# Attention scores of two transformer blocks: mask and biases added on VectorE instead of TensorE, 64-row key products padded to 128 rows

## The chip, the cores and the metric

The program runs on one core of a Trainium2 chip. The metric is device time in microseconds (us); runs of this kernel lie within about 0.1% of each other. The engines are TensorE (PE, with its weight loads PEld), VectorE (DVE), ScalarE (ACT), GpSimd (POOL) and SyncE (SP), each with its own instruction queue; they meet through semaphores.

## What is computed

Two transformer blocks on 256 tokens of width 2048, in fp32. Cut to the attention, which is what the change touches:

```python
# first block: 16 MLA heads (128 plain + 64 rotated dimensions) and 16 FoX heads (128 dimensions)
s = q @ k.T * Dk ** -0.5                    # Dk = 192 (MLA) or 128 (FoX)
s = s + F[t] - F[s']                        # FoX only: cumulative log of the forget gates
s = where(key <= query, s, -inf)
y = softmax(s) @ v
# first block goes on: gates, output projection, 16384 experts (PEER)

# second block, two layers: 4 differential heads, 8 dilated heads, a convolution
s_c = q_c @ k_c.T * 64 ** -0.5 + bias[dist] # c = 0, 1: two score maps of 64 dimensions per head
a = softmax(s_0) - lam * softmax(s_1);  y = rms_norm(a @ v)
s = q @ k.T * 128 ** -0.5 + bias[dist] + log(count of patterns)   # dilated heads, 128 dimensions
y = softmax(s) @ v
```

## The kernel before

Almost all of the program is a list of jobs. A job takes a weight block of 512 by 512 numbers from DRAM (1 MB) and cuts it into four pieces of 128 by 512. ACT rounds a piece to a high part `hi` (L204), DVE subtracts to get the low part `lo` (L205), and PE multiplies: for each of two token blocks the three products hi*h, lo*h, hi*l (L256, L257, L259), so six matmuls of 512 columns per piece. Pieces are converted up to `PIECES` = 7 ahead of the matmuls. SP loads the next blocks.

Everything else (norms, heads, rotations, the convolution) is a generator in a task list. After each piece the planner (`Tasks.step`) lets one task per lane take one step if it is due; what the step issues is then queued on the engines behind what is there. A step that yields a number waits for so many pieces; a bare `yield` waits four. PE's queue is thus a stream of main matmuls with short runs of other matmuls, called sites here, between two pieces.

An attention head is three sites. The first makes the score tile `sc` in PSUM with `qk` (first block, L561 to L569) or `qk_plain` (second block, L1092 to L1094): queries 0 to 127 against keys 0 to 127, and queries 128 to 255 against keys 0 to 255, 384 columns in all. An fp32 matmul stands in the trace as two records. In the first block `qk` adds the forget sums with a 48-row matmul (`extra`, L593: three copies of 16 rows, picked by `sel`) and the causal mask with a bf16 matmul of the identity and the mask (L569). An MLA head has a second product for its 64 rotated dimensions; two heads share one transposed tile of 128 rows, so the head takes rows 0 to 63 or 64 to 127 of it (`rows`, in `mla_group`). The differential heads take their two maps in the same way from a tile of 128 rows (`rows`, in `diff_post`).

Behind the site, `softmax_block` takes the maxima on DVE (L521, L522), negates them (L523), and ACT makes the exponentials and their sums (L524, L525). In the second block `biased` first adds the position bias on DVE from PSUM into SBUF (L1088, L1089), so that the maxima and exponentials read SBUF there and PSUM in the first block. The second site (four or more pieces later) transposes the weights, the third multiplies by the values.

POOL's queue carries the small loads of the first block: the forget bias, a triangle of ones, and the gate biases (L712). A task `forget_work` makes the forget sums `F` once.

## Time and profile before

| | |
|---|---|
| median of 3 runs | 3363.84 us (3362.52 to 3364.47) |
| profiled execution | 3362.86 us, of which the span of the trace is 3361.1 us |
| PE busy | 99% of the span |
| PEld, DVE, ACT, POOL busy | 81%, 70%, 53%, 17% |
| chain that ended last | PE 95%, DVE 3%, ACT 1%, DMA 1%, issue 1% |
| mean granted TensorE clock | 0.997 of full speed |

The page shows busy shares and the chain of work that ended last. A busy PE is not PE at its peak, since matmuls overlap in its pipeline: a record of a main matmul lasts about 0.39 us, but the next one starts 0.23 us after it. What a matmul costs the stream is therefore read from the distance of the starts in the timeline, not from the length of a record.

### The profile page before, as it was taken

The page shows a single profiled execution, that of the slowest core. Times are in us where ns is not written, and L with a number is a line of the kernel's source. Part 1 is how long each engine was busy: PE and PEld are TensorE (multiplying, and loading weights), DVE is VectorE, ACT ScalarE, POOL GpSimd, SP SyncE. Part 2 cuts the span into 40 slices and gives each one's busy share as a digit, 9 for nine tenths or more (in the row PEclk, how much of TensorE's full clock was granted, in tenths as well). Part 3 has the DMA queues.
Part 4 walks back from the last instruction along what each step waited for, and adds up shares of the span by engine and source line. Part 5 has one row for each costly group of instructions (what it writes and reads, how often), then busy time and mean ns, then how long its engine had stood idle before and what let it go on. Part 6 is the DMA issues. An engine that isn't in the chain of part 4 may idle for free.

```text
span 3361.1 us, 43418 instructions
## 1 busy us (share of the span) xinstructions
PE 3327.9 (99%) x15371; PEld 2737.1 (81%) x15372; DVE 2338.2 (70%) x4597; ACT 1772.8 (53%) x3117; POOL 558.1 (17%) x489
## 2 busy tenths in 40 slices
PE   9999999999999999999999999999999999999997
PEld 7877888888888888888888888888887888788886
DVE  6676676666778877444567677767668777778877
ACT  6655554554555555555554444444555454455453
POOL 0000000000007777877021111110000000000001
PEclk9999999999999999999999999999999999999999
DMA  6434444578547777777676666665564445444454
GB/s 241 163 138 155 174 163 164 192 236 286 197 176 213 210 198 213 213 207 213 235 276 240 247 237 237 237 240 214 198 220 163 163 170 199 173 162 161 176 188 138
DMA packets 157754, 674.46 MB, mean 201 GB/s; under 512 B 50384, under 2 KB 67152, under 8 KB 85984
## 3 DMA queue, kind: packets, MB, share of 16 engines
q1 hardware_dynamic: 102416, 613.06, 51.9%
q0 software_dynamic: 54688, 58.33, 7.3%
q8 instruction: 120, 1.97, 0.2%
q14 instruction: 98, 0.80, 0.1%
q10 hardware_dynamic: 432, 0.29, 0.0%
HBM read 633.48 MB, written 38.14 MB: 200 GB/s over the span
## 4 chain that ended last, share of the span: by engine, by line
PE 95%; DVE 3%; ACT 1%; DMA 1%; issue 1%; SPq 0%; DVEq 0%; ACTq 0%
PE acc L256 29%; PE acc L259 29%; PE acc L257 29%; PE side L226 2%; PE side L566 1%; DVE lo L205 1%; PE side L1094 1%; DMA raw<-in_win_dram 1%; PE side L531 0%; PE side L540 0%; PE side L541 0%; PE side L542 0%; PE side L569 0%; PE side L593 0%; PE side L832 0%
## 5 line engine op out<-in xcount | busy, mean ns | idle before, releaser
L205 DVE TENSOR_TENSOR lo<-raw,hi 128x512 fp32r<-128x512 f32 x2244 | 1505.4, 688 | 787.9 <-ACT hi L204 779.5
L204 ACT CAST hi<-raw 128x512 fp32r<-128x512 f32 x2244 | 1371.4, 622 | 1140.9 <-DVE lo L205 621.5
L256 PE MATMUL acc<-hi,xh 128*128 128x512 f32 x2816 | 1120.7, 398 | 2.0 <-ACT xh L1350 0.9
L259 PE MATMUL acc<-hi,xl 128*128 128x512 f32 x2816 | 1099.4, 391 | 3.0 <-DVE xl L205 2.8
L257 PE MATMUL acc<-lo,xh 128*128 128x512 f32 x2816 | 1098.7, 390 | 3.5 <-DVE lo L205 3.5
L256 PE MATMUL acc<-hi,s 128*128 128x512 f32 x1664 | 653.2, 393 | 0.6 <-ACT hi L204 0.6
L257 PE MATMUL acc<-lo,s 128*128 128x512 f32 x1664 | 647.8, 389 | 0.6 <-DVE lo L205 0.6
L259 PE MATMUL acc<-hi,s 128*128 128x512 f32 x1664 | 646.3, 390 | 0.0
L259 PEld LDWEIGHTS acc<-hi,xl 128*128 128x128 f32 x2816 | 529.3, 188 | 116.7 <-DVE xl L205 4.1
L256 PEld LDWEIGHTS acc<-hi,xh 128*128 128x128 f32 x2816 | 529.9, 188 | 112.6 <-issue 5.7
L257 PEld LDWEIGHTS acc<-lo,xh 128*128 128x128 f32 x2816 | 530.3, 188 | 109.2 <-DVE lo L205 5.5
L907 POOL DMA_INDIRECT gd<-pick x256 | 427.4, 1669 | 93.0 <-issue 74.5
L259 PEld LDWEIGHTS acc<-hi,s 128*128 128x128 f32 x1664 | 312.3, 188 | 65.4
L257 PEld LDWEIGHTS acc<-lo,s 128*128 128x128 f32 x1664 | 312.6, 188 | 64.3 <-DVE lo L205 1.3
L256 PEld LDWEIGHTS acc<-hi,s 128*128 128x128 f32 x1664 | 312.6, 188 | 64.2 <-ACT hi L204 1.5
L1327 POOL TENSOR_TENSOR X<-X,s 128x512 f32<-128x512 f32 x6 | 9.0, 1528 | 888.7 <-ACT X L1326 888.7
L1215 DVE SCALAR_TENSOR_TENSOR s<-s,vec,s 128x256 f32<-128x256 f32 x240 | 115.4, 481 | 4.6
L712 POOL DMA_DIRECT2D s<-in_bgate_dram x8 | 4.3, 538 | 676.4 <-ACT hi L204 421.4
L945 POOL DMA_DIRECT2D s<-ad x32 | 17.1, 534 | 482.6 <-PE acc L259 482.6
L937 POOL DMA_DIRECT2D ad<-s x32 | 27.4, 857 | 403.4 <-ACT s L935 403.4
L226 PE MATMUL side<-cst,s 128*128 128x128 f32 x720 | 92.6, 272 | 0.0
L226 PEld LDWEIGHTS side<-cst,s 128*128 128x128 f32 x720 | 83.6, 140 | 10.7
(269 smaller groups left out, 1807.0 us busy)
## 6 DMA issues: line engine op xcount, KB each, us to landing
raw<-in_ut_dram SPq DMA_DIRECT2D x128, 1024.0 KB, 4.9
raw<-in_pv_dram SPq DMA_DIRECT2D x128, 1024.0 KB, 4.8
raw<-in_w_dram SPq DMA_DIRECT2D x120, 1024.0 KB, 4.8
raw<-in_win_dram SPq DMA_DIRECT2D x87, 1024.0 KB, 5.0
raw<-in_wout_dram SPq DMA_DIRECT2D x32, 1024.0 KB, 5.0
raw<-in_wo_dram SPq DMA_DIRECT2D x32, 1024.0 KB, 4.8
gd<-s SPq DMA_DIRECT2D x16, 1024.0 KB, 8.7
raw<-in_wpq_dram SPq DMA_DIRECT2D x16, 1024.0 KB, 4.8
```

The lines of the kernel that those rows point to most:

```text
L204: A.copy(out=hi, in_=src)
L205: V.tensor_tensor(out=lo, in0=src, in1=hi.bitcast(F32), op=OP.subtract)
L226: PE.transpose(pv[:, i, tb * P:(tb + 1) * P], src_of(c + i, tb), ident)
L256: PE.matmul(ps[tb], lhsT=lh[:, kc, t], rhs=wh, start=start, stop=False)
L257: PE.matmul(ps[tb], lhsT=lh[:, kc, t], rhs=wl, start=False, stop=False)
L259: PE.matmul(ps[tb], lhsT=ll[:, kc, t], rhs=wh, start=False, stop=stop)
L566: PE.matmul(o, lhsT=q[:, q0:q0 + P], rhs=k[:, 0:k1], start=i == 0, stop=False)
L907: G.indirect_dma_start(out=gd.rearrange("p (n o) -> (p n) o", o=1), out_offset=bass.IndirectOffsetOnAxis(ap=pick[:, 1, h, k:k + 1].bitcast ...
L937: G.dma_start(out=S["ad", g], in_=aT.rearrange("p j t -> p (j t)"))
L945: G.dma_start(out=aT.rearrange("p j t -> p (j t)"), in_=S["ad", g])
L1094: PE.matmul(sc[:, o0:o0 + k1], lhsT=q[:, q0:q0 + P], rhs=k[:, 0:k1], start=True, stop=True)
L1215: V.scalar_tensor_tensor(out=cv[:, c], in0=pad[:, k:k + T], scalar=tapw(k), in1=cv[:, c], op0=OP.mult, op1=OP.add)
```

## The change

The forget sums are written to DRAM once (`fd`), and for each group of four FoX heads a new task, `forget_bias`, loads them back spread over all 128 partitions and adds the mask. The MLA heads get a fixed mask tile `causal`. Every score tile is then read by one DVE instruction per part that adds mask or bias, writes the sum to SBUF and keeps its maximum; ACT's exponentials read SBUF everywhere. The 48-row and the identity matmuls go. For the 64-row products the key side is stored twice, multiplied by a column `halves` that is 1 on one half of the rows and 0 on the other, and the product runs over all 128 rows.

```diff
-    identb = kept([128], BF16, "identb")
-    maskb = kept([128], BF16, "maskb")
-    V.tensor_copy(out=identb, in_=ident)
-    V.tensor_copy(out=maskb, in_=maskf)
+    causal = kept([384], name="causal")
+    V.memset(causal[:, 128:256], 0.0)
+    for c0 in (0, 256):
+        V.tensor_copy(out=causal[:, c0:c0 + 128], in_=maskf)
+    halves = kept([2], name="halves")
+    V.tensor_reduce(out=halves, in_=ident.rearrange("p (a b) -> p a b", a=2), axis=AX.X, op=OP.add)
...
-        F = kept([T], F32R, "F", 48)
-        A.activation(out=F, in_=pf, func=AF.Copy, scale=-1.0)
-        V.scalar_tensor_tensor(out=F[32:48], in0=pf[32:48], scalar=-1.0, in1=F[32:48].bitcast(F32), op0=OP.mult,
-                               op1=OP.subtract)
-        S["F"] = F
+            PE.matmul(pf, lhsT=lf[:, tb], rhs=tri[:, tb, :], start=tb == 0, stop=tb == TB - 1)
+        F = s2([T])
+        A.activation(out=F[0:16], in_=pf, func=AF.Copy, scale=-1.0)
+        G.dma_start(out=S["fd"], in_=F[0:16])
+        yield END
+
+    def forget_bias(g):
+
+        f, f0 = s4([4, T]), s2([4, P])
+        G.dma_start(out=f.rearrange("p h t -> p (h t)"), in_=row_bcast(S["fd"], 4 * g * T, 4 * T))
+        yield 8
+        mask = maskf[:, None, :].to_broadcast([P, 4, P])
+        V.tensor_tensor(out=f0, in0=f[:, :, 0:P], in1=mask, op=OP.add)
+        V.tensor_tensor(out=f[:, :, P:T], in0=f[:, :, P:T], in1=mask, op=OP.add)
+        S["fbias", g] = (f0, f)
         yield END
...
-    def softmax_block(src, sums, nmax, fresh=False):
-
-        pr = s2([384]) if fresh else src
-        mx = small(2)
-        V.tensor_reduce(out=mx[:, 0:1], in_=src[:, 0:128], axis=AX.X, op=OP.max)
-        V.tensor_reduce(out=mx[:, 1:2], in_=src[:, 128:384], axis=AX.X, op=OP.max)
+    def softmax_block(sc, b0, b1, sums):
+
+        pr = s2([384])
+        mx, nmax = small(2), small(2)
+        parts = ((slice(0, 128), b0), (slice(128, 384), b1))
+        for i, (c, bias) in enumerate(parts):
+            V.tensor_tensor_reduce(out=pr[:, c], in0=sc[:, c], in1=bias, scale=1.0, scalar=-3.0e38, op0=OP.add,
+                                   op1=OP.max, accum_out=mx[:, i:i + 1])
...
-    def qk(sc, parts, extra=None):
+    def qk(sc, parts):
 
         for q0, k1, o0 in ((0, P, 0), (P, T, P)):
-            o = sc[:, o0:o0 + k1]
             for i, (q, k) in enumerate(parts):
-                PE.matmul(o, lhsT=q[:, q0:q0 + P], rhs=k[:, 0:k1], start=i == 0, stop=False)
-            if extra:
-                extra(o, k1)
-            PE.matmul(o[:, k1 - P:k1], lhsT=identb, rhs=maskb, start=False, stop=True)
+                PE.matmul(sc[:, o0:o0 + k1], lhsT=q[:, q0:q0 + P], rhs=k[:, 0:k1], start=i == 0,
+                          stop=i == len(parts) - 1)
...
+            keys["f"] = tasks.add(forget_bias(g), [S["forget_t"]])
...
-                S["yf_t", g].append(tasks.add(head(h), [keys["q"], keys["k"], S["forget_t"]]))
+                S["yf_t", g].append(tasks.add(head(h), [keys["q"], keys["k"], keys["f"]]))
...
-        def rope_T(src):
-
-            dst = s2([2, T])
+        def rope_T(src, apart):
+
+            dst = s4([2, 2, T]) if apart else s2([2, T])
             sv = src.rearrange("p b h d -> p b (h d)")
             for pv, c in transposed(lambda c, tb: sv[:, tb, c * P:(c + 1) * P], 2):
-                A.copy(out=dst, in_=pv)
+                if not apart:
+                    A.copy(out=dst, in_=pv)
+                for i in range(2 if apart else 0):
+                    copy_scaled(dst[:, :, i], pv, halves[:, i:i + 1])
             return dst
...
-                rows, pair = slice(64 * (h % 2), 64 * (h % 2) + 64), h // 2
-                parts = [(qT[:, h], kT[:, h]), (qr[rows, pair], kr[rows, pair])]
-                yield from attention(lambda sc: qk(sc, parts), v, y, h)
+                parts = [(qT[:, h], kT[:, h]), (qr[:, h // 2], kr[:, h // 2, h % 2])]
+                yield from attention(parts, causal[:, 0:128], causal[:, 128:384], v, y, h)
...
-    def biased(ps, h):
-
-        bt = S["bias"][h // 4]
-        sb = s2([384])
-        V.tensor_tensor(out=sb[:, 0:128], in0=ps[:, 0:128], in1=bt[:, h % 4, 128:256], op=OP.add)
-        V.tensor_tensor(out=sb[:, 128:384], in0=ps[:, 128:384], in1=bt[:, h % 4, :], op=OP.add)
-        return sb
...
+    def head_bias(h):
+        bt = S["bias"][h // 4][:, h % 4]
+        return bt[:, 128:256], bt
...
+                    if name != "ak":
+                        L[name] = to_heads(raw, gain)
+                    else:
+                        L[name] = [s4([4, T]), s4([4, T])]
+                        for pv, c in transposed(lambda c, tb: raw[:, tb, c * P:(c + 1) * P], 4):
+                            for i in range(2):
+                                copy_scaled(L[name][i][:, c:c + 2, :], pv, halves[:, i:i + 1])
...
-                    rows = slice(64 * c, 64 * c + 64)
                     sc = side()
-                    qk_plain(sc, q[rows, h], k[rows, h])
-                    sb = biased(sc, h)
-                    sums, nmax, r = small(2), small(2), small(2)
-                    prs.append(softmax_block(sb, sums, nmax))
+                    qk(sc, [(q[:, h], k[c][:, h])])
+                    sums, r = small(2), small(2)
+                    prs.append(softmax_block(sc, *head_bias(h), sums))
```

PE's queue at the first FoX head, before. The score tile is `side_1466`; rows of the main stream stand ahead and behind.

```order
L259 MATMUL acc_1439<-hi_1376,s_103_468 128x512
L566 MATMUL side_1466<-s_307_1363,s_260_1156 128x128
L593 MATMUL side_1466<-F_1000,sel_915 128x128
L569 LDWEIGHTS identb_92
L569 MATMUL side_1466<-maskb_93,identb_92 128x128
L566 MATMUL side_1466<-s_307_1363,s_260_1156 128x256
L593 MATMUL side_1466<-F_1000,sel_915 128x256
L569 LDWEIGHTS identb_92
L569 MATMUL side_1466<-maskb_93,identb_92 128x128
L256 MATMUL acc_1438<-hi_1386,s_102_467 128x512
```

The same place after (the line numbers are those of the changed kernel).

```order
L261 MATMUL acc_1443<-lo_1379,s_102_469 128x512
L263 MATMUL acc_1443<-hi_1378,s_103_470 128x512
L576 MATMUL side_1470<-s_308_1365,s_259_1155 128x128
L576 MATMUL side_1470<-s_308_1365,s_259_1155 128x256
L260 MATMUL acc_1442<-hi_1390,s_102_469 128x512
L261 MATMUL acc_1442<-lo_1391,s_102_469 128x512
```

Two products are left of six matmuls. On PE no site has moved: all 290 stand between the same two main matmuls in both programs.

DVE's queue where the same head's maxima are taken, before:

```order
L205 TENSOR_TENSOR lo_1457<-raw_1276,hi_1456 128x512
L521 TENSOR_REDUCE sm_1477<-side_1466 128x1
L522 TENSOR_REDUCE sm_1477<-side_1466 128x1
L523 TENSOR_SCALAR sm_1474<-sm_1477 128x2
L551 RECIPROCAL sm_1475<-sm_1473 128x2
L205 TENSOR_TENSOR lo_1485<-raw_1276,hi_1484 128x512
```

And after; `s_287_1271` and `s_288_1272` are the group's forget sums with the mask, made by two additions (L475, L476) that stand seven `lo` pieces ahead of these rows.

```order
L209 TENSOR_TENSOR lo_1461<-raw_1278,hi_1460 128x512
L531 ISA s_336_1475,sm_1476<-side_1470,s_288_1272 128x128
L531 ISA sm_1476 128x1
L531 ISA s_336_1475,sm_1476<-side_1470,s_287_1271 128x256
L531 ISA sm_1476 128x1
L533 TENSOR_SCALAR sm_1477<-sm_1476 128x2
L562 RECIPROCAL sm_1474<-sm_1473 128x2
L209 TENSOR_TENSOR lo_1485<-raw_1278,hi_1484 128x512
```

Each part is one long instruction and a short one that writes the maximum; the `lo` pieces around them keep their places.

## Rows read from the trace of the kernel before

**Rows 1.** The page: busy us, share of span, instructions; the chain by engine.
```profile
PE 3327.9 (99%) x15371; PEld 2737.1 (81%) x15372; DVE 2338.2 (70%) x4597; ACT 1772.8 (53%) x3117; POOL 558.1 (17%) x489
...
PE 95%; DVE 3%; ACT 1%; DMA 1%; issue 1%; SPq 0%; DVEq 0%; ACTq 0%
```
**Rows 2.** Timeline of PE, a FoX head: start us, length us, line, operation.
```profile
137.87 0.39 PE L259 MATMUL acc<-hi,s 128*128 128x512 f32 x1
138.10 0.38 PE L566 MATMUL side<-s,s 128*128 128x128 f32 x2
138.41 0.32 PE L593 MATMUL side<-F,sel 48*128 48x128 f32 x1
...
139.98 0.39 PE L257 MATMUL acc<-lo,s 128*128 128x512 f32 x1
```
**Rows 3.** Timeline of PE, an MLA head (merged records: both 128 and 64 rows).
```profile
203.97 0.39 PE L259 MATMUL acc<-hi,xl 128*128 128x512 f32 x1
204.20 0.80 PE L566 MATMUL side<-s,s 128*128 128x128 f32 x4
...
206.56 0.39 PE L257 MATMUL acc<-lo,xh 128*128 128x512 f32 x1
```
**Rows 4.** Timeline of PE, one map of a differential head, 64 rows.
```profile
2524.65 0.39 PE L259 MATMUL acc<-hi,xl 128*128 128x512 f32 x1
2524.97 0.92 PE L1094 MATMUL side<-s,s 64*128 64x128 f32 x4
...
2526.16 0.39 PE L257 MATMUL acc<-lo,xh 128*128 128x512 f32 x1
```
**Rows 5.** Timeline of PE, a dilated head, 128 rows.
```profile
2606.30 0.39 PE L259 MATMUL acc<-hi,xl 128*128 128x512 f32 x1
2606.53 0.82 PE L1094 MATMUL side<-s,s 128*128 128x128 f32 x4
...
2607.41 0.39 PE L257 MATMUL acc<-lo,xh 128*128 128x512 f32 x1
```
**Rows 6.** Groups of PE by form: line, shape xcount | busy us, mean ns | idle.
```profile
L566 PE MATMUL side<-s,s 64*128 64x256 f32 x32 | 11.1, 428 | 0.0
...
L1094 PE MATMUL side<-s,s 64*128 64x256 f32 x32 | 9.5, 377 | 0.0
```
**Rows 7.** Groups of DVE by form, same columns.
```profile
L522 DVE TENSOR_REDUCE sm<-side 128x1 f32<-128x256 f32 x32 | 13.2, 413 | 0.0
L1089 DVE TENSOR_TENSOR s<-side,s 128x256 f32<-128x256 f32 x32 | 13.2, 413 | 0.0
...
L883 DVE TENSOR_TENSOR s<-s,ti 128x512 f32<-128x512 f32 x16 | 11.1, 692 | 0.6
...
L523 DVE TENSOR_SCALAR sm<-sm 128x2 f32<-128x2 f32 x64 | 10.8, 169 | 2.2
...
L521 DVE TENSOR_REDUCE sm<-side 128x1 f32<-128x128 f32 x32 | 9.2, 287 | 19.7 <-PE side L569 19.7
...
L1088 DVE TENSOR_TENSOR s<-side,s 128x128 f32<-128x128 f32 x32 | 9.1, 284 | 3.5 <-PE side L1094 3.5
```
**Rows 8.** Busy us by stretch: PE, PEld, DVE, ACT, POOL, granted clock, DMA, GB/s.
```profile
140.00:150.00 10.00, 10.00 (x47) 7.11 (x46) 4.48 (x15) 6.72 (x18) 0.00 (x0) 1.00 0.20 62
185.00:190.00 5.00, 2.21 (x9) 1.50 (x8) 4.66 (x15) 0.89 (x2) 0.00 (x0) 0.94 0.16 64
190.00:195.00 5.00, 5.00 (x23) 4.06 (x22) 4.62 (x17) 1.77 (x3) 0.00 (x0) 0.72 0.60 210
290.00:300.00 10.00, 10.00 (x45) 8.24 (x45) 9.49 (x26) 5.90 (x9) 0.54 (x1) 1.00 0.50 178
```
**Rows 9.** Group of ACT by form: copies of transposed heads with a scale.
```profile
L503 ACT ACTIVATE s<-side,vec 128x512 f32<-128x512 f32 x32 | 20.2, 683 | 18.5 <-PE side L226 18.5
```
**Rows 10.** DMA issues: queue, xcount, KB each, median us from issue to landing.
```profile
gd<-s SPq DMA_DIRECT2D x16, 1024.0 KB, 8.7
...
s<-in_lng_dram SPq DMA_DIRECT2D x8, 256.0 KB, 7.8
```

More of the change, by code (lines that the diff above doesn't have):

```diff
@@ L447, in forget_work @@
         G.dma_start(out=tri.rearrange("p b t -> p (b t)"), in_=a["cst"][:, 256:768])
-        z, u, lf = s2([TB, 16]), s2([TB, 16]), s2([TB, 3, 16])
-        V.memset(lf[:, :, 1, :], 0.0)
-        sel = kept([16], F32R, "sel", 48)
-        V.tensor_tensor(out=sel, in0=ident[0:48, 0:16], in1=ident[0:48, 32:48], op=OP.add)
-        S["sel"] = sel
+        z, u, lf = s2([TB, 16]), s2([TB, 16]), s2([TB, 16])
+        S["fd"] = dram.tile([16, T], F32, name="fd")
         yield
@@ L457, in forget_work @@
         A.activation(out=u, in_=u, func=AF.Ln, bias=1.0)
-        for i in (0, 2):
-            V.scalar_tensor_tensor(out=lf[:, :, i, :], in0=z, scalar=0.0, in1=u, op0=OP.min, op1=OP.subtract)
+        V.scalar_tensor_tensor(out=lf, in0=z, scalar=0.0, in1=u, op0=OP.min, op1=OP.subtract)
         yield
-        pf = side()[0:48, 0:T]
+        pf = side()[0:16, 0:T]
         for tb in range(TB):
-            PE.matmul(pf, lhsT=lf[:, tb].rearrange("p a b -> p (a b)"), rhs=tri[:, tb, :], start=tb == 0,
-                      stop=tb == TB - 1)
-        F = kept([T], F32R, "F", 48)
-        A.activation(out=F, in_=pf, func=AF.Copy, scale=-1.0)
-        V.scalar_tensor_tensor(out=F[32:48], in0=pf[32:48], scalar=-1.0, in1=F[32:48].bitcast(F32), op0=OP.mult,
-                               op1=OP.subtract)
-        S["F"] = F
+            PE.matmul(pf, lhsT=lf[:, tb], rhs=tri[:, tb, :], start=tb == 0, stop=tb == TB - 1)
[11 more added lines that the diff above has]
+        S["fbias", g] = (f0, f)
         yield END
@@ L515, in fox_norm @@
         return work()
-    def softmax_block(src, sums, nmax, fresh=False):
-        pr = s2([384]) if fresh else src
-        mx = small(2)
-        V.tensor_reduce(out=mx[:, 0:1], in_=src[:, 0:128], axis=AX.X, op=OP.max)
-        V.tensor_reduce(out=mx[:, 1:2], in_=src[:, 128:384], axis=AX.X, op=OP.max)
+    def softmax_block(sc, b0, b1, sums):
[5 more added lines that the diff above has]
+                                   op1=OP.max, accum_out=mx[:, i:i + 1])
         V.tensor_scalar(out=nmax, in0=mx, scalar1=-1.0, scalar2=None, op0=OP.mult)
-        A.activation(out=pr[:, 0:128], in_=src[:, 0:128], func=AF.Exp, bias=nmax[:, 0:1], accum_out=sums[:, 0:1])
-        A.activation(out=pr[:, 128:384], in_=src[:, 128:384], func=AF.Exp, bias=nmax[:, 1:2], accum_out=sums[:, 1:2])
+        for i, (c, bias) in enumerate(parts):
+            A.activation(out=pr[:, c], in_=pr[:, c], func=AF.Exp, bias=nmax[:, i:i + 1],
+                         accum_out=sums[:, i:i + 1])
         return pr
@@ L543, in values, with attention @@
         return o
-    def attention(scores, v, y, h):
+    def attention(parts, b0, b1, v, y, h):
         sc = side()
-        scores(sc)
-        sums, nmax, rs = small(2), small(2), small(2)
-        pr = softmax_block(sc, sums, nmax, True)
+        qk(sc, parts)
+        sums, rs = small(2), small(2)
+        pr = softmax_block(sc, b0, b1, sums)
         V.reciprocal(out=rs, in_=sums)
@@ L589, in head @@
                 qT, kT = S["fq", g], S["fk", g]
-                hd = 4 * g + h
-                def extra(o, k1):
-                    PE.matmul(o, lhsT=S["sel"][:, hd:hd + 1].to_broadcast([48, P]), rhs=S["F"][:, 0:k1], start=False,
-                              stop=False)
-                yield from attention(lambda sc: qk(sc, [(qT[:, h], kT[:, h])], extra), v, y, h)
+                f0, f = S["fbias", g]
+                yield from attention([(qT[:, h], kT[:, h])], f0[:, h], f[:, h], v, y, h)
             for h in range(4):
-                S["yf_t", g].append(tasks.add(head(h), [keys["q"], keys["k"], S["forget_t"]]))
+                S["yf_t", g].append(tasks.add(head(h), [keys["q"], keys["k"], keys["f"]]))
         w = a["win"]
@@ L1171, in head @@
                     sc = side()
-                    qk_plain(sc, q[:, h], k[:, h])
-                    sb = biased(sc, 4 + 4 * b + h)
-                    sums, nmax, r = small(2), small(2), small(2)
-                    pr = softmax_block(sb, sums, nmax)
+                    qk(sc, [(q[:, h], k[:, h])])
+                    sums, r = small(2), small(2)
+                    pr = softmax_block(sc, *head_bias(4 + 4 * b + h), sums)
                     V.reciprocal(out=r, in_=sums)
```

10 lines of the change are left out of this document (3 added, 7 removed).

## The prediction

> **What bounds the kernel now.** I read the page first. PE is busy for 99% of the span and holds 95% of the chain that ended last, while DVE is busy for 70% and ACT for 53% [rows 1]. So the time is the length of PE's stream, and the question for each part of the change is how much of that stream it takes out, and whether DVE, which gets the work, can still deliver the pieces in time. Then I read PE's timeline at one site of each kind of head. The reader is to look at the starts. At an undisturbed place a main matmul starts 0.23 us after the one before it (137.87 to 138.10 [rows 2]), so a site costs the distance from the last main matmul ahead of it to the second main matmul behind it, less two times 0.23. I take the second one behind, because the first starts early and lasts longer, and hands part of the site's price to its successor.
>
> By this reading:
> - FoX head: 137.87 to 139.98 = 2.11, less 0.46 = 1.65 us [rows 2].
> - MLA head: 203.97 to 206.56 = 2.59, less 0.46 = 2.13 us [rows 3].
> - One map of a differential head, 64 rows: 2524.65 to 2526.16 = 1.51, less 0.46 = 1.05 us [rows 4].
> - Dilated head, 128 rows, nothing added on PE: 2606.30 to 2607.41 = 1.11, less 0.46 = 0.65 us [rows 5].
>
> The last two are the pair on which everything rests. They compute tiles of one shape (384 score columns, two records each), and the one with half the contracting rows costs 0.40 us **more**. A 64-row product thus does not stream faster, and something is paid when PE goes from 128 rows to fewer and back: about 0.20 us for each such change.
>
> That price also explains the other sites. In a FoX head the rows change four times (into and out of the 48-row matmul, twice): 0.65 + 4 x 0.20 = 1.45, and the remaining 0.20 is the extra columns of the forget and mask matmuls. In an MLA head: two products, 1.30, plus four changes, 0.80, makes 2.10 of 2.13.
>
> A page of the Trainium skill bears on this.
> The Trainium skill, "TensorEngine Tiling (Array Packing)", under Key Properties, says that changing the tiling mode drains TensorE, which agrees with the 0.40 us between rows 4 and rows 5. The same page, under Theoretical Speedup, speaks against the change: a product of at most 64 rows can run up to two times faster, because two tiles work side by side. By that rule a 64-row map would cost half of 0.65, about 0.33 us (an estimate from that page and rows 5), and padding 16 maps would lose 16 x 0.32 = 5 us; the trace shows 1.05 where the rule would have 0.33, since no two such products stand together here. With it the sum would be 3329 + 6.4 + 5 = 3340 us; I give it no chance of its own, as rows 4 measure the very product.
>
> **The change, part by part.**
>
> *FoX heads, 16.* The forget and mask matmuls go and the site becomes that of a dilated head: 2.11 - 1.11 = 1.00 us each, 16.0 us. All of it is PE's own stream, so it lies on the path.
>
> *MLA heads, 16* (two records of each 64-row form per head: 32 [rows 6]). The mask goes and the rotated product becomes a second product of 128 rows. The site becomes two dilated products, 2 x 0.65 = 1.30: 2.13 - 1.30 = 0.83 us each, 13.3 us.
>
> *Differential maps, 16* (again 32 records [rows 6]). 1.51 - 1.11 = 0.40 us each, 6.4 us. Dilated heads keep their site.
>
> Together 35.7 us of PE's stream. PE gets no new matmul: the transposes for the padded keys are those of before, and the matmul for the forget sums only has fewer columns of weights.
>
> *DVE, maxima.* An instruction that adds and keeps a maximum does not occur before. Below, it costs what an addition from PSUM costs: 284 + 413 ns [rows 7]. Above, the addition and the maximum as two passes: 284 + 287 + 413 + 413 = 1397 ns. Each part has a short second instruction; between nothing and 169 ns, a two-element operation. I take one pass and 0.1 us for each read-out, 0.9 us per head, since it makes one pass over the data; with both upper ends it is 1.74 us. Before, the first block's two maxima took 287 + 413 = 0.70 us. So DVE gets 0.2 us (0 to 1.04) more per head there. In the second block the two additions go as well, and DVE gains or stays level. The cover: while the first FoX heads ran, DVE was busy 4.48 us of 10 [rows 8]. The four heads stand in consecutive pieces, 6 x 0.23 + 0.65 = 2.03 us apart after the change, and per piece DVE has 0.69 for `lo`, 0.9, and two operations of 0.17: 1.93 us. That fits without touching the seven pieces of lead. At 1.74 us DVE falls 0.74 us behind per piece, 3 us over four heads, while seven pieces of lead are 9.6 us. Cost on the path: none, within bounds 0 to 5 us in all.
>
> *DVE, forget bias.* Two additions of 128x512, 0.69 us each [rows 7], per FoX group: 1.4 us, four times, seven pieces ahead of the first head. Behind them wait the `lo` pieces, and behind these PE. They wait for a load of 512 KB that was issued eight pieces, 8 x 1.38 = 11 us, earlier in program order. The nearest rows are 7.8 us for a load of the same spread kind and half the size, and 8.7 us for 1 MB [rows 10]. If it took 15 us, DVE would stand 4 us and still be inside its lead. The four loads go through POOL's queue, where gate biases stand between them; each of those waits for a buffer that an earlier piece frees, so nothing late sits in front. Cost: none, at most a few us.
>
> *ACT.* Exponentials now read SBUF instead of PSUM, 384 columns as before. An MLA group gets one more copy of 0.68 us, each differential layer two more [rows 9]. ACT has slack everywhere; where two groups of transposes stand in neighbouring pieces, PE may wait for a PSUM buffer for part of such a copy. I allow 1 us for this in all, 0 to 3.
>
> *A stall that stays.* Around 186 us PE stands still: 2.21 of 5 us busy [rows 8], so 2.8 us are lost, and the granted clock of 0.94 and 0.72 in the two stretches (the lower level, 1.2 GHz, for a while, after PE had been idle) loses 0.3 + 1.4 more: 4.5 us. DVE is then full with the first MLA group's norms and rotations (4.66 of 5). Nothing of that is changed, and I leave it in the sum.
>
> **The sum.** The profiled execution took 3362.86 us, 1.0 below the median. 3362.86 - 35.7 + 1 = 3328.2; on the median's scale 3329 us, a gain of 1.0%.
>
> **Rivals.**
>
> *DVE becomes the bound in more places.* At 290 to 300 us, where the second MLA group makes its norms, DVE is already busy 9.49 of 10 us [rows 8], and PE does not wait. With PE 4 us faster over the heads ahead of it and 2 to 5 us more on DVE, the lead may be used up there, and the stall of 186 us (4.5 us) is repeated in up to three more groups. Against it: between the heads and that stretch DVE has time to catch up. Result: 3329 + 3 x 4.5 = 3342 us.
>
> *Padding doesn't take the price out of the MLA site.* If the 0.8 us there came from a second product into the same scores and not from the change of rows, only the mask would go: about 0.1 us x 16 instead of 13.3. Result: 3329 + 11.7 = 3341 us. Against it: the four prices above agree within 0.03 us.
>
> *The add-with-maximum is far dearer than any row* (slower). DVE's budget per head piece, with the lead spent over four heads, is 0.9 + 0.1 + 9.6 / 4 = 3.4 us. Beyond that, PE waits one for one for the excess, 32 heads of the first block alone. The gain is gone when the excess is 35.7 / 32 = 1.1 us: from 4.5 us per head on, five times my price, the kernel is slower. At 5 us it loses 51 - 36 = 15 us: 3379 us. Nothing in the trace prices such an instruction above two passes.
>
> *Nothing moves* (3358 to 3370): the same mechanism between 4.3 and 4.7 us, or several of the above together.
>
> **Chances.** Forecast, 3322 to 3338: 0.78. DVE stalls repeated, 3338 to 3345: 0.11. MLA price stays: 0.05. No change: 0.03. Slower: 0.03. The range that should hold the time 8 times in 10 goes from 3322 (the stall at 186 us gone, and 2 us more) to 3342, which takes in the first two rivals. A difference under 0.2%, 6.7 us, can't be told from no change here. Faster: 0.78 + 0.11 + 0.05 = 0.94; same 0.03; slower 0.03.
>
> **What would show it.** In the changed trace, read as above, FoX, differential and dilated sites should all cost 0.65 us and MLA sites 1.30. The long add-with-maximum instructions should last about 0.28 and 0.41 us and the short ones about 0.1. The waits of PE for `lo` should still be the one near 182 us. The forecast is wrong if an MLA site stays above 1.6 us, if DVE's long instruction takes over 1 us, or if new gaps in front of `lo` stand behind the FoX groups' additions (a late load) or in the second to fourth MLA group.

## Result: 3319.5 us, a gain of 1.3% where 1.0% was forecast

The changed kernel takes 3319.48 us (median; 3319.21 to 3320.63), the kernel before 3363.18 us (3362.35 to 3364.47). The ratio is 0.987, with a 95% interval of 0.9853 to 0.9887. The direction was right, but the gain of 43.7 us is 9 us larger than forecast: the time lies 2.5 us below the low end of the range, 3322. So the question for the runs is not why the change helps but where 9 us came from that no term of the sum held.

The page of the changed kernel, with the columns of [rows 1]:

```profile
PE 3288.9 (99%) x15275; PEld 2734.3 (82%) x15276; DVE 2324.9 (70%) x4667; ACT 1779.5 (54%) x3125; POOL 559.3 (17%) x494
...
PE 98%; DVE 2%; issue 0%; ACT 0%; DMA 0%; DVEq 0%; SPq 0%
```

PE bounds the kernel as it did, and its share of the chain rose from 95 to 98%. DVE was given additions and yet is busy for 13 us less (2338.2 before). The lines of the main matmuls are now L260, L261, L263, those of `hi` and `lo` L208 and L209, and all score products stand in L576.

PE's timeline at a FoX head (answers to [rows 2]), an MLA head ([rows 3]) and a differential map ([rows 4]), read as the prediction reads them:

```profile
137.00 0.39 PE L263 MATMUL acc<-hi,s 128*128 128x512 f32 x1
137.23 0.81 PE L576 MATMUL side<-s,s 128*128 128x128 f32 x4
...
138.11 0.39 PE L261 MATMUL acc<-lo,s 128*128 128x512 f32 x1
...
199.15 0.39 PE L263 MATMUL acc<-hi,xl 128*128 128x512 f32 x1
199.38 1.47 PE L576 MATMUL side<-s,s 128*128 128x128 f32 x8
...
200.92 0.40 PE L261 MATMUL acc<-lo,xh 128*128 128x512 f32 x1
...
2494.97 0.39 PE L263 MATMUL acc<-hi,xl 128*128 128x512 f32 x1
2495.20 0.82 PE L576 MATMUL side<-s,s 128*128 128x128 f32 x4
...
2496.09 0.39 PE L261 MATMUL acc<-lo,xh 128*128 128x512 f32 x1
```

FoX: 138.11 - 137.00 - 0.46 = 0.65 us. MLA: 1.77 - 0.46 = 1.31. Differential: 1.12 - 0.46 = 0.66. Forecast were 0.65, 1.30 and 0.65. Over all sites the medians are 0.661 and 1.317 us.

The new instruction, groups of DVE by form (busy us, mean ns of one):

```profile
L531 DVE CUSTOM_DVE_ANT_0 s<-side,s 128x256 f32<-128x256 f32 x48 | 20.2, 420 | 0.0
L531 DVE CUSTOM_DVE_ANT_0 s<-side,s 128x128 f32<-128x128 f32 x48 | 13.7, 286 | 5.3 <-PE side L576 5.3
L531 DVE DVE_READ_ACCUMULATOR2_ANT sm<- 128x1 f32 x128 | 10.7, 84 | 0.0
```

An addition that keeps the maximum makes one pass: 286 and 420 ns, against 284 and 413 for a bare addition [rows 7]. The Trainium skill, "VectorE: DVE Perf Modes", section "Two Vector instructions with no wait between them", says that an operation which also writes out its accumulator is two instructions; the trace agrees, with 128 reads of 84 ns beside the 128 long instructions (the 32 that are not shown read `causal` and last as long).

To find the other gain I set the n-th main matmul of one trace against the n-th of the other (13440 in both) and read how the difference of their starts grows:

| stretch | forecast, us | measured, us |
|---|---|---|
| first 100 us, first loads | 0 | 0.8 |
| first block, with its 32 heads | 29.3, less part of 1 for ACT | 28.6 |
| from there to the second block | 0 | 0.3 |
| second block, first layer | 3.2 | 5.9 |
| second block, second layer | 3.2 | 6.0 |
| tail behind the last main matmul | 0 | 1.9 |

The first block came as forecast. The surplus stands in three places: 5.5 us in the second block, 1.9 us in the tail, and 0.8 us at the start. Against the same trace of before, the other kernels' traces lie between -0.5 and 1.2 us there, so the start says nothing of the change.

In the second block the trace of before has small stops of PE that are gone after. PE's timeline of before at one of them, and DVE's at the same time:

```profile
2726.53 0.39 PE L259 MATMUL acc<-hi,xl 128*128 128x512 f32 x1
2727.23 0.50 PE L256 MATMUL acc<-hi,s 128*128 128x512 f32 x1 [0.31 <-ACT hi L204]
2728.05 0.50 PE L257 MATMUL acc<-lo,s 128*128 128x512 f32 x1 [0.31 <-DVE lo L205]
```
```profile
2726.70 0.69 DVE L1246 SCALAR_TENSOR_TENSOR s<-s,s 128x512 fp32r<-128x512 f32 x1 [0.70 <-ACT s L1245]
2727.31 1.89 DVE L205 TENSOR_TENSOR lo<-raw,hi 128x512 fp32r<-128x512 f32 x3
```

The starts are 0.70 and 0.82 us apart where 0.23 is the rule: `lo` stands in DVE's queue behind the last steps of the convolution, one of which had itself waited 0.70 us for ACT. Before, each layer has five such places, 0.44 to 0.82 us from start to start; at one of them the transposes wait for ACT's exponentials, at one the products with the values wait for a step of the convolution on ACT. After, there is none. The waits of PE, engine and line waited for, us in total, times, longest; before, then after:

```profile
PE acc L257 <- DVE lo L205: 4.1, 5, 2.8
...
PE side L540 <- ACT s L1229: 0.4, 2, 0.2
PE side L531 <- ACT s L525: 0.3, 2, 0.2
```
```profile
PE acc L261 <- DVE lo L209: 3.0, 2, 2.8
PE acc L263 <- DVE xl L209: 2.8, 1, 2.8
```

The recorded waits are shorter than the losses, because the gap from start to start grows by more than the wait, and the next starts are late too. The two stops of 2.8 us that are left are old ones: the one near 181 us that the forecast left in its sum, and the one at the start of the second layer.

### The profile page after: what moved, and what is told of

The parts are those of the page before. It is cut to its first block, busy times and chain, and to the rows that moved or that the text cites. A ratio compares the mean times of both kernels' runs of the same rounds, so it can differ in the third digit from the quotient of the medians.

```text
span 3317.4 us, 43290 instructions
## 1 busy us (share of the span) xinstructions
PE 3288.9 (99%) x15275; PEld 2734.3 (82%) x15276; DVE 2324.9 (70%) x4667; ACT 1779.5 (54%) x3125; POOL 559.3 (17%) x494
## 4 chain that ended last, share of the span: by engine, by line
PE 98%; DVE 2%; issue 0%; ACT 0%; DMA 0%; DVEq 0%; SPq 0%
PE acc L263 30%; PE acc L260 30%; PE acc L261 30%; PE side L230 3%; PE side L576 2%; PE side L542 1%; PE side L552 0%; PE side L553 0%; PE side L551 0%; DVE lo L209 0%; DVE X L1318 0%; PE side L839 0%; DMA X<-in_x_dram 0%; DVE X L1323 0%; DVE lst L1304 0%
## 5 line engine op out<-in xcount | busy, mean ns | idle before, releaser
L209 DVE TENSOR_TENSOR lo<-raw,hi 128x512 fp32r<-128x512 f32 x2244 | 1506.1, 689 | 784.3 <-ACT hi L208 775.9
L208 ACT CAST hi<-raw 128x512 fp32r<-128x512 f32 x2244 | 1369.8, 622 | 1128.7 <-DVE lo L209 610.4
L260 PE MATMUL acc<-hi,xh 128*128 128x512 f32 x2816 | 1122.7, 399 | 2.0 <-ACT xh L1352 0.9
L263 PE MATMUL acc<-hi,xl 128*128 128x512 f32 x2816 | 1098.9, 391 | 2.8 <-DVE xl L209 2.8
L261 PE MATMUL acc<-lo,xh 128*128 128x512 f32 x2816 | 1098.4, 390 | 3.0 <-DVE lo L209 3.0
L260 PE MATMUL acc<-hi,s 128*128 128x512 f32 x1664 | 654.5, 393 | 0.0
L261 PE MATMUL acc<-lo,s 128*128 128x512 f32 x1664 | 647.6, 389 | 0.0
L263 PE MATMUL acc<-hi,s 128*128 128x512 f32 x1664 | 646.1, 389 | 0.0
L263 PEld LDWEIGHTS acc<-hi,xl 128*128 128x128 f32 x2816 | 529.5, 188 | 116.0 <-DVE xl L209 4.1
L261 PEld LDWEIGHTS acc<-lo,xh 128*128 128x128 f32 x2816 | 530.2, 188 | 108.3 <-DVE lo L209 4.6
L260 PEld LDWEIGHTS acc<-hi,xh 128*128 128x128 f32 x2816 | 530.2, 188 | 107.7 <-ACT xh L1352 1.6
L263 PEld LDWEIGHTS acc<-hi,s 128*128 128x128 f32 x1664 | 312.4, 188 | 65.4
L261 PEld LDWEIGHTS acc<-lo,s 128*128 128x128 f32 x1664 | 312.6, 188 | 63.3
L260 PEld LDWEIGHTS acc<-hi,s 128*128 128x128 f32 x1664 | 312.6, 188 | 63.1
L535 ACT ACTIVATE s<-s,sm 128x128 f32<-128x128 f32 (+1 forms) x128 | 57.3, 448 | 123.4 <-DVE sm L533 123.4
```

The costliest lines, as they stand in the source:

```text
L208: A.copy(out=hi, in_=src)
L209: V.tensor_tensor(out=lo, in0=src, in1=hi.bitcast(F32), op=OP.subtract)
L260: PE.matmul(ps[tb], lhsT=lh[:, kc, t], rhs=wh, start=start, stop=False)
L261: PE.matmul(ps[tb], lhsT=lh[:, kc, t], rhs=wl, start=False, stop=False)
L263: PE.matmul(ps[tb], lhsT=ll[:, kc, t], rhs=wh, start=False, stop=stop)
L535: A.activation(out=pr[:, c], in_=pr[:, c], func=AF.Exp, bias=nmax[:, i:i + 1], accum_out=sums[:, i:i + 1])
```

## The experiments

### Padding alone

```diff
...
-                rows, pair = slice(64 * (h % 2), 64 * (h % 2) + 64), h // 2
-                parts = [(qT[:, h], kT[:, h]), (qr[rows, pair], kr[rows, pair])]
+                parts = [(qT[:, h], kT[:, h]), (qr[:, h // 2], kr[:, h // 2, h % 2])]
...
-                    qk_plain(sc, q[rows, h], k[rows, h])
+                    qk_plain(sc, q[:, h], k[c][:, h])
```

This is the kernel before with the padded keys of the change, and nothing else.

> The kernel before with only the padding: the rotated key product of the MLA heads and the differential maps run over 128 rows; the forget and mask matmuls stay on TensorE, additions and maxima as before. If a price of about 0.2 us is paid at each change between 128 and fewer rows, a differential site falls from 1.05 to 0.65 us and an MLA site from 2.13 to about 1.42 (two products of 0.65 and the mask): 16 x 0.40 + 16 x 0.71 = 18 us less, about 3345 us, with the small stops of TensorE in the second block still there. Rival, that the MLA price comes from the second product into the same scores: the MLA sites stay near 2.1 and the time is about 3357 us. Rival on the unexplained 8 us: if the second block's stops went because its sites are shorter, they go here too and the time is about 3340 us.

Measured: 3351.56 us, ratio 0.9968 (0.9956 to 0.998), a gain of 11.6 us where 18 were expected. A differential site fell from 1.06 to 0.661 us, as in the changed kernel. An MLA site fell only to 1.537, by 0.60. Of the first block 9.6 us came off, but of the second only 0.7 us a layer, though its sites are 3.2 us a layer shorter. New stops took the rest, such as this one (PE's timeline; `lo` is L207 here):

```profile
2535.19 0.39 PE L258 MATMUL acc<-hi,xh 128*128 128x512 f32 x1
2536.17 0.50 PE L259 MATMUL acc<-lo,xh 128*128 128x512 f32 x1 [0.59 <-DVE lo L207]
```

So in the second block DVE had no room for a faster PE. Padding pays there only if DVE gets less to do.

### The addition on VectorE alone

```diff
...
-                parts = [(qT[:, h], kT[:, h]), (qr[:, h // 2], kr[:, h // 2, h % 2])]
+                rows, pair = slice(64 * (h % 2), 64 * (h % 2) + 64), h // 2
+                parts = [(qT[:, h], kT[:, h]), (qr[rows, pair], kr[rows, pair])]
...
-                    qk(sc, [(q[:, h], k[c][:, h])])
+                    qk(sc, [(q[rows, h], k[rows, h])])
```

The changed kernel with products of 64 rows, as they were.

> The changed kernel without the padding: masks and biases are added on VectorE with the maximum, the 64-row products stay at 64 rows. By the price of a change of rows, a FoX site is 0.65 us (1.00 less than before), an MLA site about 2.03 (only the mask gone, 0.1 less), a differential site stays at 1.05: 16.0 + 1.6 = 17.6 us of TensorE's stream, and if the second block's stops (5 us) go because VectorE has less to do there, about 3340 us. If those stops went through the padding, about 3345 us.

Measured: 3339.03 us, ratio 0.9929 (0.9914 to 0.9944), a gain of 24.1 us. FoX sites cost 0.659 us, differential ones 1.056 as before, and MLA sites 2.098: without its mask, but with 64-row products, an MLA site is only 0.04 us shorter. One of them, in PE's timeline:

```profile
200.46 0.39 PE L263 MATMUL acc<-hi,xl 128*128 128x512 f32 x1
200.69 2.05 PE L576 MATMUL side<-s,s 128*128 128x128 f32 x8
...
203.01 0.39 PE L261 MATMUL acc<-lo,xh 128*128 128x512 f32 x1
```

The second block gains 2.7 us a layer although none of its sites is shorter.

The two parts alone give 11.6 + 24.1 = 35.7 us, together 43.7. The sum is 8 us short of the whole. About 5 us of that stand in the second block: 0.7 and 2.7 us a layer alone, 5.9 and 6.0 together. The next two runs turn DVE's work there. Another 2.4 us stand in the first block, at the MLA sites: padding takes 2.135 - 1.537 = 0.60 us off a site that has its mask and 2.098 - 1.317 = 0.78 off one that has none, and 16 x 0.18 = 2.9 us, a little more than is missing. The second kernel also has a stop of 1.9 us at 189 us, from start to start, that the changed kernel has not, but it is no loss between the two: the granted clock is 1.00 there over 180 to 190 us and 0.83 in the changed kernel, and from 130 to 200 us both gain 4.0 and 3.9 us on the kernel before.

### One instruction or two in the second block

Two kernels turn the same thing in both directions. The first takes the changed kernel and splits the addition and the maximum in the second block; the second takes the kernel before and joins them there.

```diff
...
+        for i, (c, bias) in enumerate(parts):
+            V.tensor_tensor(out=pr[:, c], in0=sc[:, c], in1=bias, op=OP.add)
+        for i, (c, bias) in enumerate(parts):
+            V.tensor_reduce(out=mx[:, i:i + 1], in_=pr[:, c], axis=AX.X, op=OP.max)
...
-                    prs.append(softmax_block(sc, *head_bias(h), sums))
+                    prs.append(softmax_two(sc, *head_bias(h), sums))
...
```

> The changed kernel, but in the second block the bias is added by one VectorE operation and the maximum taken by a second one, as before; TensorE's stream is that of the changed kernel. Theory, that 5 us of the gain came from VectorE's shorter work in the second block: TensorE's stops ahead of the transposes, of the convolution's products and behind them come back, about 2.5 us per layer, and the time is about 3324 to 3326 us (3319.5 for the changed kernel). Rival, that the stops went with the shorter sites: no change, 3319 to 3320 us.

Measured: 3330.38 us, ratio 0.9904 (0.9889 to 0.9919), 11 us over the changed kernel and 4 us over the upper end of what was expected. Some 1.4 us of the 11 came behind an old stop at the start of the second layer, where the granted clock is 0.83 over 2845 to 2865 us and 0.91 at the same place of the changed kernel. The old stops are back, and there are new ones at the differential heads, which padding had made shorter. One of them, in PE's and in DVE's timeline:

```profile
2515.29 0.40 PE L260 MATMUL acc<-hi,xh 128*128 128x512 f32 x1
2516.27 0.50 PE L261 MATMUL acc<-lo,xh 128*128 128x512 f32 x1 [0.58 <-DVE lo L209]
```
```profile
2515.13 0.48 DVE L1161 SCALAR_TENSOR_TENSOR s<-s,sm,s 128x256 f32<-128x256 f32 x1
2515.53 0.68 DVE L209 TENSOR_TENSOR lo<-raw,hi 128x512 fp32r<-128x512 f32 x1
```

DVE works without a pause and delivers `lo` late. PE waits for `lo` eleven times, 7.1 us in all, where the changed kernel has two waits. The forecast for this run counted only the old stops; it missed that the shorter sites ask `lo` sooner, as in the first run.

```diff
...
-                    sb = biased(sc, h)
-                    sums, nmax, r = small(2), small(2), small(2)
-                    prs.append(softmax_block(sb, sums, nmax))
+                    sums, r = small(2), small(2)
+                    prs.append(softmax_one(sc, *head_bias(h), sums))
...
```

> The kernel before, but in the second block bias and maximum are one VectorE operation; TensorE's instructions are those of before, 64-row products included. Theory, that VectorE's work makes the stops in the second block: about 5 us less, 3358 us, with all sites at their old price. Rival, that they go with the sites: no change, 3363 us.

Measured: 3357.37 us, ratio 0.9984 (0.9975 to 0.9993), a gain of 5.7 us. No site and no product of PE is changed, and each layer is 2.7 to 2.8 us shorter. Five places hold 2.5 us of it in the first layer: 0.23 us behind 2585.86, 0.64 at 2623.45, 0.48 at 2707.83, and 0.47 and 0.70 at the two starts of 2727 and 2728 shown above. They are the stops of the kernel before. This is the missing term by itself: 5.5 us from DVE's shorter work. With the 3.2 us of its sites it makes the 5.9 us a layer of the table.

### One instruction or two in the first block

```diff
...
-        pr = softmax_block(sc, b0, b1, sums)
+        pr = softmax_two(sc, b0, b1, sums)
```

The changed kernel, with the addition and the maximum split in the first block's 32 heads.

> The changed kernel, but in the first block (FoX and MLA heads) mask or bias is added by one VectorE operation and the maximum taken by a second one: 0.7 us more VectorE work per head, 32 heads. In the second block, with the convolution beside the heads, the same exchange cost 11 us. If in the first block VectorE has room beside the heads, nothing is lost here: 3319 to 3321 us. Rival, that the one-instruction form is worth as much here: 3325 to 3330 us.

Measured: 3327.96 us, ratio 0.9897 (0.988 to 0.9913), 8.5 us over the changed kernel. The rival held; the cover that the prediction spoke of does not exist at this price. All score sites still cost what they do in the changed kernel. What is new is a wait of the transposes for the exponentials. PE's waits, PE's timeline at one of four stops of 1.4 us, and DVE's timeline just ahead of it:

```profile
PE side L557 <- ACT s L550: 5.1, 10, 1.0
```
```profile
418.18 0.40 PE L263 MATMUL acc<-hi,s 128*128 128x512 f32 x1
419.59 0.33 PE L557 MATMUL side<-cst,s 128*128 128x128 f32 x1 [1.02 <-ACT s L550]
```
```profile
414.16 0.61 DVE L545 TENSOR_TENSOR s<-side,s 128x128 f32<-128x128 f32 x2
414.70 0.60 DVE L547 TENSOR_REDUCE sm<-s 128x1 f32<-128x128 f32 x2
...
416.55 0.17 DVE L577 RECIPROCAL sm<-sm 128x2 f32<-128x2 f32 x1 [1.05 <-ACT s L550]
417.06 0.69 DVE L209 TENSOR_TENSOR lo<-raw,hi 128x512 fp32r<-128x512 f32 x1 [0.34 <-ACT hi L208]
417.67 0.62 DVE L545 TENSOR_TENSOR s<-side,s 128x128 f32<-128x128 f32 x2
```

The rows show a ring through two queues. DVE's maxima release ACT's exponentials; the reciprocal behind the maxima waits for them (1.05 us); `lo` waits for `hi`, which stands on ACT behind the exponentials (0.34 us); and the next head's maxima stand behind `lo`. One turn takes 417.67 - 414.16 = 3.51 us, though DVE is idle for 1.4 us of it. The same ring in the changed kernel, DVE's timeline:

```profile
408.63 0.29 DVE L531 CUSTOM_DVE_ANT_0 s<-side,s 128x128 f32<-128x128 f32 x1
...
410.53 0.17 DVE L562 RECIPROCAL sm<-sm 128x2 f32<-128x2 f32 x1 [1.05 <-ACT s L535]
411.04 0.69 DVE L209 TENSOR_TENSOR lo<-raw,hi 128x512 fp32r<-128x512 f32 x1 [0.34 <-ACT hi L208]
411.65 0.28 DVE L531 CUSTOM_DVE_ANT_0 s<-side,s 128x128 f32<-128x128 f32 x1
```

A turn takes 3.02 us here, and took 2.98 in the kernel before, where PE needed 3.03 us from head to head. Now PE needs 2.04 us (403.56 to 405.60), so even the changed kernel falls a microsecond behind at every head, and lives on the distance from the scores to the transposes. The fourth head of this group has its exponentials at 416.44 and its transposes start at 416.86: 0.42 us are left. With 0.49 us more in each of four turns, 1.96 us, less the 0.42, some 1.5 us must appear as a stop. The rows show 419.59 - 418.18 - 0.23 = 1.2 us ahead of the first transpose, and the next ones wait too: read from start to start, this site of transposes is 1.62 us dearer than in the changed kernel. The four sites with such a stop (418, 506, 635 and 701 us) are 6.2 us dearer together, two others (151 and 270 us) 0.9, and the products with the values behind them 1.0; that is 8.1 of the 8.5 us.

### The price of changing rows

Two kernels take the row changes out of the kernel before without taking a product out. In the first the forget matmul contracts 128 rows, of which 80 are zeros; in the second an MLA head's products are ordered 128, mask, 64, 64, 128, mask, so that the rows change twice and not four times.

```diff
...
-        z, u, lf = s2([TB, 16]), s2([TB, 16]), s2([TB, 3, 16])
-        V.memset(lf[:, :, 1, :], 0.0)
-        sel = kept([16], F32R, "sel", 48)
+        z, u, lf = s2([TB, 16]), s2([TB, 16]), s2([TB, 8, 16])
+        V.memset(lf, 0.0)
+        sel = kept([16], F32R, "sel")
...
-        F = kept([T], F32R, "F", 48)
+        F = kept([T], F32R, "F")
...
```

> The kernel before, but the forget matmul of the FoX heads contracts 128 rows, 80 of them zero, in place of 48; nothing else moves. If the price of a FoX site is the change between 128 and 48 rows (four times 0.2 us), it falls from 1.65 to about 1.05 us: the plain products 0.66, the forget matmul's own columns 0.16, and the two mask matmuls, which cost 0.22 in an MLA site whose products all have 128 rows. 16 x 0.6 = 10 us less, about 3353 us. Rival, that the price is the two extra matmuls as such: no change, 3363 us.

Measured: 3353.25 us, ratio 0.9972 (0.9962 to 0.9983), a gain of 9.2 us. PE's timeline at the head of [rows 2]:

```profile
137.20 0.39 PE L259 MATMUL acc<-hi,s 128*128 128x512 f32 x1
...
137.56 0.31 PE L593 MATMUL side<-F,sel 128*128 128x128 f32 x1
...
138.74 0.39 PE L257 MATMUL acc<-lo,s 128*128 128x512 f32 x1
```

1.54 - 0.46 = 1.08 us against 1.65: more rows, the same six products, and 0.56 us less by the medians (1.656 to 1.092).

```diff
-            for i, (q, k) in enumerate(parts):
-                PE.matmul(o, lhsT=q[:, q0:q0 + P], rhs=k[:, 0:k1], start=i == 0, stop=False)
+            todo = [lambda i=i: PE.matmul(o, lhsT=parts[i][0][:, q0:q0 + P], rhs=parts[i][1][:, 0:k1], start=i == first,
+                                          stop=len(parts) > 1 and i != first and q0 == 0) for i in range(len(parts))]
+            first = 1 if len(parts) > 1 and q0 > 0 else 0
...
+            todo[first]()
+            if len(parts) > 1 and q0 == 0:
+                mask(False)
+                todo[1]()
+                continue
...
```

> The kernel before, with the matmuls of an MLA site in another order: the 64-row product of the first 128 queries comes last and that of the second 128 queries first, so that both 64-row products stand together and the rows change twice per site in place of four times. Theory of a price per change: about 0.35 to 0.4 us less per site, less about 0.1 for a mask that no longer hides in a change, 4 to 6 us in all, 3357 to 3359 us. Rival, a price per 64-row matmul whatever stands beside it: no change, 3363 us.

Measured: 3359.24 us, ratio 0.999 (0.9981 to 1.0), a gain of 3.3 us, at the edge of what can be told from no change. The site itself is clear: 2.135 to 1.870 us, 0.27 for two changes fewer; 16 of them are 4.2 us.

Where no mask product stands at the site, a change of rows costs 0.395 / 2 = 0.20 us at a differential map and 0.78 / 4 = 0.20 at an MLA head (the second run against the changed kernel). Where the masks are there, taking a change out gives less: 0.60 / 4 = 0.15 us by padding and 0.27 / 2 = 0.13 by the order at an MLA head, 0.56 / 4 = 0.14 at a FoX head. At the MLA head the runs show why: the site's two masks cost 1.537 - 1.317 = 0.22 us when all products have 128 rows and 2.135 - 2.098 = 0.04 when the rows change next to them, so 0.18 us of their work comes back when the changes go. That the same holds at the FoX head is likely and not shown; no run has a 48-row product without the masks. The Trainium skill, "TensorEngine Tiling (Array Packing)", section Key Properties, says that a change of mode drains TensorE; these runs agree, and add the price.

### The stop near 181 us

```diff
...
-                    yield
+                    yield 30 if b else None
...
```

The changed kernel, in which the second half of the MLA queries' rotation may be issued thirty pieces later.

> The changed kernel, with the rotation of the second half of the MLA queries (heads 8 to 15, six VectorE operations of 0.69 us) done 30 pieces later in place of right behind that of the first half. If VectorE's backlog makes TensorE stop at 181 us (2.8 us idle and 1.4 us at the lower clock behind it), that stop goes: about 4 us less than the changed kernel, 3315 to 3316 us. Rival, that the stop comes from the first MLA group's own norms: it stays, 3319 to 3320 us.

Measured: 3316.56 us (3315.5 to 3316.61), ratio 0.9862 (0.9846 to 0.9879), the fastest of all kernels here; its range and that of the changed kernel do not overlap. PE's timeline at the stop, in the changed kernel and in this one:

```profile
180.96 0.39 PE L260 MATMUL acc<-hi,xh 128*128 128x512 f32 x1
184.16 0.75 PE L261 MATMUL acc<-lo,xh 128*128 128x512 f32 x1 [2.82 <-DVE lo L209]
184.72 0.63 PE L263 MATMUL acc<-hi,xl 128*128 128x512 f32 x1
185.14 0.63 PE L260 MATMUL acc<-hi,xh 128*128 128x512 f32 x1
```
```profile
184.90 0.48 PE L260 MATMUL acc<-hi,xh 128*128 128x512 f32 x1
186.10 0.50 PE L261 MATMUL acc<-lo,xh 128*128 128x512 f32 x1 [0.72 <-DVE lo L209]
186.44 0.39 PE L263 MATMUL acc<-hi,xl 128*128 128x512 f32 x1
186.67 0.39 PE L260 MATMUL acc<-hi,xh 128*128 128x512 f32 x1
```

The stop is 1.2 us and not 3.2 from start to start, and behind it the matmuls start 0.23 us apart at once, where the changed kernel has 0.43 for the next seven (the granted clock is 0.74 over 185 to 190 us: part of that at the lower level, 1.2 GHz). The first block gains 3.9 us. Some 1.2 us of it are lost again at the start of the second layer, where the granted clock is 0.83 over 20 us and 0.91 in the changed kernel; the stop became shorter and did not go, and the time is 0.6 us above the upper end of what was expected.

### The tail

From the start of the last main matmul to the end of the span, the kernel before takes 19.4 us and the changed one 17.5, though the last block's code is the same. What the change adds to POOL's queue are five transfers in the first block: the write of the forget sums and the four loads. Two kernels turn this in both directions: the kernel before with these five transfers added, read by nobody, and the changed kernel with them issued from ACT's queue.

```diff
+        S["fd"] = dram.tile([16, T], F32, name="fd")
+        G.dma_start(out=S["fd"], in_=F[0:16].bitcast(F32))
...
+        f = s4([4, T])
+        G.dma_start(out=f.rearrange("p h t -> p (h t)"), in_=row_bcast(S["fd"], 4 * g * T, 4 * T))
...
```

> The kernel before with the five transfers of the changed kernel added on POOL's queue (the forget sums written to DRAM, and four loads of 512 KB, which nothing reads). PE's stream is unchanged. The question is the tail, from the last PE instruction to the end of the span: 19.35 us in the kernel before, 17.46 us in the changed one. Theory that the transfers on POOL's queue decide it: tail 17.4 to 17.6 us, time about 1.9 us under the kernel before, 3361.3. Rival, that something else in the first block's code decides it (fewer instructions on PE, other buffers): tail 19.3 to 19.4 us, time as before, 3362 to 3365.

```diff
-        G.dma_start(out=S["fd"], in_=F[0:16])
+        A.dma_start(out=S["fd"], in_=F[0:16])
...
-        G.dma_start(out=f.rearrange("p h t -> p (h t)"), in_=row_bcast(S["fd"], 4 * g * T, 4 * T))
+        A.dma_start(out=f.rearrange("p h t -> p (h t)"), in_=row_bcast(S["fd"], 4 * g * T, 4 * T))
```

> The changed kernel with the same five transfers issued from ACT's queue instead of POOL's. Theory that POOL's transfers decide the tail: tail back at 19.3 to 19.4 us, time about 1.9 us over the changed kernel, 3321.4, if the waits that the issues put into ACT's queue cost nothing. Rival: tail stays at 17.4 to 17.6 us, time 3319 to 3320.

Measured: 3360.62 us, ratio 0.9993 (0.9983 to 1.0003), for the kernel before with the transfers, and 3321.79 us, ratio 0.9878 (0.9862 to 0.9894), for the changed kernel without them on POOL. The times differ by 2.5 and 2.3 us in the expected directions, the first within what can't be told from no change; the traces are plainer. POOL's last work in the kernel before, the changed one, and these two, in this order (timelines of POOL):

```profile
3350.78 3.28 POOL L1327 TENSOR_TENSOR X<-X,s 128x512 f32<-128x512 f32 x2 [1.51 <-ACT X L1326]
```
```profile
3309.00 3.28 POOL L1329 TENSOR_TENSOR X<-X,s 128x512 f32<-128x512 f32 x2 [1.52 <-ACT X L1328]
```
```profile
3351.69 3.28 POOL L1336 TENSOR_TENSOR X<-X,s 128x512 f32<-128x512 f32 x2 [1.51 <-ACT X L1335]
```
```profile
3309.41 3.28 POOL L1329 TENSOR_TENSOR X<-X,s 128x512 f32<-128x512 f32 x2 [1.51 <-ACT X L1328]
```

The spans are 3361.1, 3317.4, 3360.1 and 3319.7 us. Behind POOL's last instruction follow 7.0, 5.1, 5.1 and 7.0 us. The tail goes with the five transfers on POOL's queue, over 2700 us ahead of it, in both directions, and so it does in all twelve traces: 17.45 to 17.48 us with them, 19.34 to 19.35 without. POOL's closing instruction, a DRAIN, lasts 8.87 us without the transfers on POOL and 5.40 us with them. Without them POOL's last semaphore steps start 0.05 us behind its end; with them 1.6 us pass, so something other than the drain holds the end there, and 1.9 of the 3.5 us show in the time. Why the drain depends on transfers so long before, and whether each of the five counts or only their number, stays open.

## Why the prediction was right, and where it failed

**What bounds the kernel, and the sites: right.** PE's stream sets the time, and all three site forecasts hold to 0.02 us: 0.661 (0.65), 1.317 (1.30), 0.661 (0.65). The sites' 35.7 us were 35.3.

**The price of a change of rows: right, but the FoX site was divided wrongly.** The prediction explained three sites by 0.20 us for each change. Where no mask stands beside the change the runs give 0.20, and the MLA sum holds in its parts: two products and four changes were to cost 2.10 us, and 2.098 is what the site costs without its mask. At the FoX head the prediction gave the forget and mask matmuls 0.20 us; among products of 128 rows they cost 1.092 - 0.661 = 0.43, and the four changes gave back only 0.56 us and not 0.80. The FoX gain held all the same because the site was read whole and both causes went at once. The second rival, that padding would not help the MLA site, is refuted by the first run.

**The new instruction: right.** One pass, 0.286 and 0.420 us. The instructions overlap: both parts with their reads take from 408.63 to 409.28, 0.65 us, where 0.9 was taken.

**The cover in the first block: right result, wrong argument.** The prediction added up DVE's busy time, 1.93 us in 2.03, and called the rest lead. The ring shows that a head takes DVE and ACT 3.02 us, waits included, so there was a shortage already. It cost nothing because the ring hardly became slower than before (2.98) and four heads are just too few to use up the distance to the transposes: 0.42 us of it were left. The upper bound of 5 us for two passes was too low: 8.5 us.

**The forget bias and ACT's copies: right, nearly nothing.** The four loads landed within 3.4 to 5.4 us of their issue, and no `lo` was late for them. The first block came 0.4 us short of the 29.0 us that its sites measured, against 1 us allowed.

**The stall that stays: right.** It stood in the same place, at 3.2 us from start to start, and moving one task took most of it away. The lower clock behind it, which the prediction priced as 1.7 us on top, is not a loss by itself: in three kernels here (the second run, the one with the MLA order, the one with the loads on ACT) the granted clock did not fall behind the stop, PE stopped again for 1.9 us instead, and by 200 us they had lost as much as their nearest kernels within 0.1 us.

**DVE in the second block "gains or stays level": here the step failed.** The prediction put this term at nothing. It asked only whether DVE's work could add stops and not whether stops were there that less work would remove, although the trace of before has them, five in a layer. PE's 99% hid them: the five lose some 2.5 us in a layer of 475 (2585.86 to its like at 3061.05). A head's DVE work fell from 1.4 to 0.65 us, and 5.5 us came with it, as the run that joins the instructions in the second block alone shows. Without it, the padding there would have been worth 0.7 us a layer and not 3.2, as the first run shows.

**The tail** gave 1.9 us that nothing in the prediction spoke of, the start 0.8 us that are noise. 34.7 + 5.5 + 1.9 + 0.8 + 0.6 = 43.5 of 43.7 us; the 0.6 are 0.3 in the first block and 0.3 behind it, by which these came out better than the forecast less its 1 us for ACT. The 5.5 us alone would have left the time at 3323.5, inside the range; with the tail and the start it fell out. The range's low end allowed for one gain, the stall at 186 us; that did not come, and two others did.

## What to carry to other kernels

A bounding engine that is 99% busy can still stop often and shortly: before an edit gives work to its feeder or takes work from it, list the gaps between its starts, and price those that would go as well as those that would come. Where two in-order queues feed each other (maxima, exponentials, and the pieces queued behind both), compare the length of one turn with the pace of the bounding engine, not the busy time. A lone product over fewer rows in a stream of 128-row products is not cheaper; filling it with zeros to 128 took 0.4 to 0.8 us off each site here. Price such a piece with its neighbours as they will stand: the masks looked nearly free only as long as the rows changed next to them.

## What was not expected of the hardware

- The time at the end of the program depends on POOL's transfers long before: 7.0 us behind POOL's last instruction without the five extra transfers, 5.1 us with them, in two kernels each.
- The two bf16 mask products of a site, 128 columns each, cost 0.22 us together among products of 128 rows, and 0.04 us where the rows change next to them.
- The granted clock fell to the lower level, 1.2 GHz, during or behind the same stop of 2.8 us (its start between 181 and 186 us) in eight traces and not in three.
- The instruction that adds and keeps a maximum from PSUM costs only 2 to 7 ns more than the addition alone.
